# A 64-wide recurrence on TensorE: block-diagonal operands of two heads against 64x64 quarters

## The chip, the core and the metric

The kernel runs on one core of one Trainium2 chip. The metric is the device time in microseconds of one execution. Engines are called TensorE (PE in the profile, its weight loads PEld), VectorE (DVE), ScalarE (ACT), GpSimd (POOL) and SyncE (SP). L229 is line 229 of the kernel before.

## What is computed

One decoder layer over 512 tokens of width 1024: an input projection, two groups of heads side by side (eight RWKV-7 heads of width 64 and eight block-sparse attention heads), an output projection, a layer norm, 32 routed experts and a second norm. The change concerns the RWKV-7 heads, whose reference is a scan over tokens:

```python
def step(S, inp):
    rt, wt, kt, vt, at, bt = inp
    sa = jnp.einsum('bhij,bhj->bhi', S, at)
    S = S * wt[:, :, None, :] + sa[..., None] * bt[:, :, None, :] + vt[..., None] * kt[:, :, None, :]
    yt = jnp.einsum('bhij,bhj->bhi', S, rt)
    return S, yt
```

with `at = -kk`, `bt = kk * a`, and S a 64x64 state per head. All is computed in fp32; the large projections split each operand into two parts.

## The kernel before

The tokens are cut into 8 chunks of 64. Within a chunk the recurrence becomes dense algebra: masked products of the chunk's vectors, the inverse of a unit triangular 64x64 matrix, and products with that inverse; the state then goes from chunk to chunk. Two heads make a pair (`hp`, four of them) and lie on partitions 0 to 63 and 64 to 127.

For each pair there are four stages. `feat` (L399) projects keys, receptances and values (three projections of 24 products with 512 moving columns, L356) and makes the operands AR and BK, held in one of two slots, so that the next pair's may be made while the last is in use. `pre` (L543) works on all 8 chunks: it copies BK into block-diagonal operands (L550 to L554), so that one 128x128 product serves both heads; multiplies (L569, L571) and masks (L572 to L580); inverts the diagonal 16-blocks by substitution, 15 rounds of a shuffle, a product and a sum on VectorE (L583 to L587); transposes the operands on TensorE and copies them out in 64-row pieces, on VectorE and ScalarE (L592 to L605); and doubles the inverse from 16 to 32 and to 64, in two groups of 4 chunks (L616 to L653). L655 to L664 make what the state of each chunk needs. `chain` (L669) runs over the chunks: a transpose of the state, a scaled copy on ScalarE (L683), one product, and additions on VectorE (L688, L689). `gnorm` (L692) normalizes.

All products go through the helper at L229, transposes through L232, whose records carry no other line; which stage one belongs to is seen from its neighbours and its tiles. The program is written stage by stage, and a scheduler lays each engine's instructions in an order by priority. `early` (L725) gives `feat` of the next pair a priority 200 instructions ahead of its place and `pre` one of 100 ahead, so on TensorE the projections of the next pair lie between the products of this one. Each engine then runs its list strictly in order. The work buffers of `pre` are freed at its end and reused by the next pair's. The projections of the attention (L476) and the attention itself (L505) come after; they fill TensorE from about 250 us on. The experts follow from about 500 us.

Of the kernel before, what the change touches and what calls it, by code (L numbers as in the profile page):

```python
# [12 lines left out]
AF = mybir.ActivationFunctionType  # L13
OP = mybir.AluOpType
# [10 lines left out]
    ("tri", 130), ("bdone", 128), ("i64", 64), ("m16d", 64), ("minc", 64),  # L25
    ("mstr", 128), ("m16", 128), ("m32", 128), ("d16", 16), ("bm16", 8), ("hsel", 4),
# [5 lines left out]
def const_array(which):  # L32
# [14 lines left out]
    c["m16d"] = (s[:, None] // 16 == t[None, :] // 16) & (s[:, None] < t[None, :])  # L47
    c["minc"] = s[:, None] <= t[None, :]
    c["mstr"] = same * (s[:, None] < s[None, :])
    c["m16"] = same * ((s[:, None] // 32 == s[None, :] // 32) & (s[:, None] % 32 < 16) & (s[None, :] % 32 >= 16))  # L50
    c["m32"] = same * ((s[:, None] < 32) & (s[None, :] >= 32))
    c["d16"] = (p[:, None] % 16 == np.arange(16)[None, :])
    c["bm16"] = (p[:, None] // 16 == np.arange(8)[None, :])
# [132 lines left out]
def layer(ctx: ExitStack, tc: tile.TileContext, xT, xt, wb, wad, pc, wla, al, gl, cst, cst2, cst3, abias, wout,  # L186
# [199 lines left out]
    CH = [(T(128), T(128)) for _ in range(2)]  # L386
# [155 lines left out]

    def pre(hp, W, RB):  # L543
        d = st[hp]
        AR, BK = v3(d["AR"].f, 8), v3(d["BK"].f, 8)
        BD = [T(1024, *W) for _ in range(2)]
        bd = [v3(t.f, 8) for t in BD]
        at("pa", hp)
        for w in range(2):
            P.memset(bd[w][0:64, :, 64:128], 0.0)  # L550
            P.memset(bd[w][64:128, :, 0:64], 0.0)
            for h in range(2):
                q = slice(64 * h, 64 * h + 64)
                S.activation(bd[w][q, :, q], BK[q, :, 64 * w:64 * w + 64], AF.Copy)  # L554
        T16, T32, RB_, KB_, VB, RH = (T(1024, *W) for _ in range(6))
        AkT = T(1024, *W)
        t16, t32, arb, ark, vb, rh, akt = (v3(t.f, 8) for t in (T16, T32, RB_, KB_, VB, RH, AkT))
        Tc, z, zt = T(128, *W), T(128, *W), T(128, *W)
        tc3, z3, zt3 = (v3(t.f, 8) for t in (Tc, z, zt))
        pr = T(256, *W)  # L560
        P.memset(vb[0:64, :, 64:128], 0.0)
        P.memset(vb[64:128, :, 0:64], 0.0)
        at("pb", hp)
        for g in range(2):
            cs = slice(4 * g, 4 * g + 4)
            pa, pk = bank(RB), bank(RB)
            pa4, pk4 = v3(pa, 4), v3(pk, 4)
            for c in range(4):
                mm(pa4[:, c, :], bd[0][:, 4 * g + c, :], AR[:, 4 * g + c, 0:128])  # L569
            for c in range(4):  # L570
                mm(pk4[:, c, :], bd[1][:, 4 * g + c, :], AR[:, 4 * g + c, 0:128])  # L571
            V.tensor_tensor(v3(pr.f, 4), pa4[:, :, 64:128], bc(cc("m16d"), 4), op=OP.mult)  # L572
            V.tensor_reduce(tc3[:, cs, :], pr.f.rearrange("p (c q t) -> p c t q", c=4, q=4), axis=AX.X, op=OP.add)
            for dst, src, m in ((t16, pa4, "m16"), (t32, pa4, "m32"), (akt, pk4, "mstr")):
                V.tensor_tensor(dst[:, cs, :].rearrange("p c (h t) -> p c h t", h=2),
                                src[:, :, None, 64:128].to_broadcast([128, 4, 2, 64]),
                                cc(m).rearrange("p (h t) -> p h t", h=2)[:, None].to_broadcast([128, 4, 2, 64]),
                                op=OP.mult)
            V.tensor_tensor(arb[:, cs, 0:64], pa4[:, :, 0:64], bc(cc("minc"), 4), op=OP.mult)
            V.tensor_tensor(ark[:, cs, 0:64], pk4[:, :, 0:64], bc(cc("minc"), 4), op=OP.mult)  # L580

        at("pc", hp)
        V.tensor_copy(z3, bc(cc("d16"), 8))  # L583
        for s in range(15):
            V.stream_shuffle(zt3[:, :, s + 1:], tc3[:, :, s + 1:], [16 * (j // 16) + s for j in range(32)])  # L585
            V.tensor_tensor(zt3[:, :, s + 1:], zt3[:, :, s + 1:], z3[:, :, s:s + 1].to_broadcast([128, 8, 15 - s]), op=OP.mult)  # L586
            V.tensor_tensor(z3[:, :, s + 1:], z3[:, :, s + 1:], zt3[:, :, s + 1:], op=OP.add)  # L587
        at("pd", hp)
        for g in range(2):
            cs = slice(4 * g, 4 * g + 4)  # L590

            for src, o, d0, d1 in ((BK, 0, arb, ark), (AR, 64, rh, vb)):  # L592
                pt = bank(RB)
                pt4 = v3(pt, 4)
                for c in range(4):
                    tp(pt4[:, c, :], src[:, 4 * g + c, o:o + 128])
                for w, dst in enumerate((d0, d1)):
                    q = slice(64 * w, 64 * w + 64)
                    for h, o_ in ((0, 0 if dst is vb else 64), (1, 64)):
                        o_ = 0 if dst is rh else o_  # L600
                        qd = slice(64 * h, 64 * h + 64)
                        if h:
                            V.tensor_copy(dst[qd, cs, o_:o_ + 64], pt4[q, :, 64:128])  # L603
                        else:
                            S.activation(dst[qd, cs, o_:o_ + 64], pt4[q, :, 0:64], AF.Copy)  # L605
            pv = bank(RB)
            for c in range(4):
                mm(v3(pv, 4)[:, c, :], akt[:, 4 * g + c, :], vb[:, 4 * g + c, :])
            S.activation(rh[0:64, cs, 64:128], v3(pv, 4)[0:64, :, 0:64], AF.Copy)
            V.tensor_copy(rh[64:128, cs, 64:128], v3(pv, 4)[64:128, :, 64:128])  # L610
        at("pe", hp)
        for t in (AkT, pr, zt, Tc, *BD):
            t.free()
        qg, oh = AR, BK
        bufs, G = [], []
        for g in range(2):  # L616
            cs = slice(4 * g, 4 * g + 4)
            Z, X, Y, WB = T(512, *W), T(512, *W), T(512, *W), T(1024, *W)
            bufs += [Z, X, Y, WB]
            P.tensor_tensor(Z.f.rearrange("p (c q t) -> p c q t", c=4, q=8),  # L620
                            z3[:, cs, None, :].to_broadcast([128, 4, 8, 16]),
                            cc("bm16")[:, None, :, None].to_broadcast([128, 4, 8, 16]), op=OP.mult)
            wb5 = WB.f.rearrange("p (c w h j) -> p c w h j", c=4, w=2, h=2)
            P.memset(wb5[0:64, :, :, 1, :], 0.0)
            P.memset(wb5[64:128, :, :, 0, :], 0.0)
            G.append((g, cs, Z, X, Y, v3(Z.f, 4), v3(X.f, 4), v3(Y.f, 4), wb5, v4(WB.f, 4, 2)))

        def both(banks, work, evac):
            for g, cs, Z, X, Y, z4, x4, y4, wb5, w4 in G:
                ps = B[RB[banks[g]]]  # L630
                for c in range(4):
                    work(v3(ps, 4)[:, c, :], c, 4 * g + c, z4[:, c, :], x4[:, c, :], y4[:, c, :])
                evac(ps, g, Z, X, Y)

        def copy(g, o, i):
            if g == 0:
                S.activation(o, i, AF.Copy)
            else:
                V.tensor_copy(o, i)

        for g, cs, Z, X, *_ in G:
            V.transpose(X.f, Z.f)
        both((2, 0), lambda o, c, k, z, x, y: mm(o, t16[:, k, :], x), lambda ps, g, Z, X, Y: copy(g, Y.f, ps))
        both((1, 2), lambda o, c, k, z, x, y: mm(o, y, z),
             lambda ps, g, Z, X, Y: V.tensor_tensor(Z.f, ps, Z.f, op=OP.add))  # L645
        both((0, 1), lambda o, c, k, z, x, y: mm(o, z, rh[:, k, :], start=(c == 0), stop=False),
             lambda ps, g, Z, X, Y: copy(g, X.f, ps))
        both((2, 2), lambda o, c, k, z, x, y: mm(o, t32[:, k, :], x), lambda ps, g, Z, X, Y: copy(g, Y.f, ps))
        both((0, 1), lambda o, c, k, z, x, y: mm(o, z, y, start=False), lambda *a: None)
        for g, cs, Z, X, Y, z4, x4, y4, wb5, w4 in G:  # L650
            p14 = B[RB[g]].rearrange("p (c w j) -> p c w j", c=4, w=2)
            S.activation(wb5[0:64, :, :, 0, :], p14[0:64], AF.Copy)
            V.tensor_copy(wb5[64:128, :, :, 1, :], p14[64:128])  # L653
        at("pf", hp)
        for g, cs, Z, X, Y, z4, x4, y4, wb5, w4 in G:  # L655
            pq, po = (B[RB[2]], B[RB[0]]) if g == 0 else (B[RB[1]], B[RB[2]])
            for c in range(4):
                mm(v3(pq, 4)[:, c, :], w4[:, c, 0, :], arb[:, 4 * g + c, :])
            for c in range(4):
                mm(v3(po, 4)[:, c, :], w4[:, c, 1, :], arb[:, 4 * g + c, :], stop=False)  # L660
                mm(v3(po, 4)[:, c, :], vb[:, 4 * g + c, :], ark[:, 4 * g + c, :], start=False)
# [4 lines left out]
        for t in bufs + [z, T16, T32, RB_, KB_, VB, RH]:  # L666
            t.free()
# [959 lines left out]
```

## Time and profile before

| | |
|---|---|
| median of 3 runs | 770.71 us (768.93 to 770.89) |
| the profiled execution | 770.63 us, span 768.9 us |
| TensorE busy in the span | 668.0 us, 87% |
| VectorE busy | 429.8 us, 56% |
| ScalarE busy | 250.1 us, 33% |
| GpSimd busy | 193.6 us, 25% |
| TensorE's granted clock, mean | 0.927 of full speed |
| share of the chain of waits: TensorE, VectorE, DMA | 54%, 24%, 17% |

The profile holds one execution. A record of TensorE lasts from its start until its last result, and the next one starts before that, so busy time is more than the time its work needs; the distance from start to start tells the pace. The chain of waits goes back from the last instruction to what released each one. The granted clock is TensorE's, as a share of 2.4 GHz; its lower level is half of that.

### The profile page before, as it was taken

Reading aid. Unit: us, or ns where it says so; the run is one execution under the profiler, and the core shown is the slowest. Engines: PE = TensorE matmul, PEld = TensorE weight load, DVE = VectorE, ACT = ScalarE, POOL = GpSimd, SP = SyncE. Lnnn points to the kernel's source line nnn. Section 1 sums busy time; section 2 is a strip of 40 time slices with the busy share of each in tenths; the row PEclk is TensorE's granted clock in tenths of the full one; section 3 lists DMA queues with packets and bytes.
Section 4 is the critical chain, followed back from the end, with each engine's and each line's share of the span. In section 5 each row is a group of like instructions: output and inputs, shape, how many; then the busy total and the mean of one; then the engine's idle time right before and its main releaser. Section 6 shows DMA issues by size and latency. Waiting matters only on the chain.

```text
span 768.9 us, 9702 instructions
## 1 busy us (share of the span) xinstructions
PE 668.0 (87%) x3420; PEld 421.4 (55%) x3420; DVE 429.8 (56%) x1243; ACT 250.1 (33%) x525; POOL 193.6 (25%) x198
## 2 busy tenths in 40 slices
PE   8988978879889899899999997499999897879870
PEld 2766866677778577667767676333333232223340
DVE  4488588868777985572444498821221121202975
ACT  4333324233333345461453343121322121201330
POOL 3133341353253220310211052611121110101432
PEclk9989999989898999999999997599999998977995
DMA  8611000000100113340637446489999999999603
GB/s 321 256 55 55 29 29 27 29 28 28 28 29 14 56 40 99 93 163 1 246 110 261 181 160 262 160 311 421 427 420 425 425 422 423 423 422 406 258 3 113
DMA packets 28484, 147.18 MB, mean 191 GB/s; under 512 B 5113, under 2 KB 5625, under 8 KB 20492
## 3 DMA queue, kind: packets, MB, share of 16 engines
q1 hardware_dynamic: 23676, 134.61, 45.0%
q0 software_dynamic: 4608, 11.62, 3.9%
q8 instruction: 29, 0.48, 0.3%
q14 instruction: 27, 0.22, 0.1%
q10 hardware_dynamic: 144, 0.26, 0.1%
HBM read 138.38 MB, written 15.36 MB: 200 GB/s over the span
## 4 chain that ended last, share of the span: by engine, by line
PE 54%; DVE 24%; DMA 17%; issue 2%; ACT 1%; POOL 1%; SPq 0%; DVEq 0%; ACTq 0%; POOLq 0%
PE bank L229 49%; DMA b<-in_wex 13%; PE bank L232 4%; DMA a<-in_wex 4%; DVE base L586 2%; DVE base L587 2%; DVE a L147 1%; DVE base L1392 1%; DVE b L603 1%; DVE base L585 1%; DVE a L460 1%; DMA a<-in_xT 1%; DVE base L1214 1%; DVE base L242 1%; DVE base L688 1%
## 5 line engine op out<-in xcount | busy, mean ns | idle before, releaser
L229 PE MATMUL bank<-a,b 128*128 128x512 f32 (+2 forms) x1112 | 286.5, 455 | 12.8 <-DMA a<-in_wex 12.0
L229 PEld LDWEIGHTS bank<-a,b 128*128 128x128 f32 (+1 forms) x1112 | 158.1, 175 | 95.4 <-issue 50.3
L229 PE MATMUL bank<-b,base 128*64 128x512 f32 (+1 forms) x412 | 92.7, 497 | 8.7 <-DMA b<-in_wex 5.1
L337 POOL TENSOR_TENSOR b<-b,b 128x1024 fp32r<-128x1024 f32 x22 | 52.4, 2382 | 131.5 <-ACT b L336 131.2
L1226 DVE SCALAR_TENSOR_TENSOR base<-bank,base 128x256 f32<-128x256 f32 x16 | 7.7, 483 | 126.2 <-ACT base L1225 126.2
L229 PE MATMUL bank<-a,base 128*64 128x512 f32 (+3 forms) x308 | 75.7, 570 | 3.0 <-DMA a<-in_wex 1.9
L229 PEld LDWEIGHTS bank<-b,base 128*64 128x64 f32 (+1 forms) x412 | 41.7, 163 | 47.8 <-issue 34.1
L229 PE MATMUL bank<-a 128*128 128x128 f32 (+4 forms) x248 | 55.6, 333 | 5.5 <-DVE base L243 2.5
L229 PEld LDWEIGHTS bank<-a,base 128*64 128x64 f32 (+2 forms) x308 | 24.3, 143 | 46.8 <-issue 37.3
L1225 ACT ACTIVATE base<-bank 128x256 f32<-128x256 f32 x16 | 6.1, 384 | 132.3 <-PE bank L229 132.3
L229 PEld LDWEIGHTS bank<-a 128*128 128x128 f32 (+1 forms) x248 | 36.0, 190 | 18.3 <-issue 5.3
L229 PE MATMUL bank<-a,a 128*128 128x128 f32 (+2 forms) x200 | 42.6, 346 | 1.4 <-DVE base L243 1.1
L232 PE MATMUL bank<-base 128*128 128x128 f32 x156 | 30.1, 293 | 10.7 <-DVE base L689 5.7
L232 PEld LDWEIGHTS bank<-base 128*128 128x128 f32 x156 | 18.1, 143 | 38.3 <-issue 16.2
L229 PEld LDWEIGHTS bank<-a,a 128*128 128x128 f32 x200 | 32.2, 213 | 8.7 <-issue 5.1
L229 PE MATMUL bank<-base 128*128 128x36 f32 (+4 forms) x136 | 28.3, 344 | 8.4 <-DVE base L1062 3.2
L232 PE MATMUL bank<-base,a 128*128 128x128 f32 x168 | 31.7, 289 | 0.0
L229 PE MATMUL bank<-b,a 128*128 128x128 f32 x192 | 29.9, 298 | 1.7 <-DVE a L645 0.9
L336 ACT ACTIVATE b<-b 128x1024 fp32r<-128x1024 f32 x25 | 26.3, 1055 | 13.5 <-PE bank L229 6.7
L1316 POOL DMA_INDIRECT ydram<-x,base x13 | 13.1, 1011 | 67.1 <-ACT base L1231 56.1
L229 PEld LDWEIGHTS bank<-b,a 128*128 128x128 f32 x192 | 27.0, 211 | 3.9 <-DVE a L645 1.9
L520 DVE CUSTOM_DVE_ANT_0 a<-bank,a 128x512 f32<-128x512 f32 (+3 forms) x32 | 15.6, 488 | 20.9 <-PE bank L232 13.7
(311 smaller groups left out, 1010.5 us busy)
## 6 DMA issues: line engine op xcount, KB each, us to landing
a<-in_wex SPq DMA_DIRECT2D x28, 2048.0 KB, 30.6
b<-in_wex SPq DMA_DIRECT2D x30, 1024.0 KB, 26.5
b<-in_wb SPq DMA_DIRECT2D x25, 512.0 KB, 3.3
a<-in_wex SPq DMA_DIRECT2D x16, 512.0 KB, 15.0
ydram<-base SPq DMA_DIRECT2D x1, 4096.0 KB, 15.2
a<-ydram POOLq DMA_DIRECT2D x4, 1024.0 KB, 14.4
x<-in_wout SPq DMA_DIRECT2D x6, 512.0 KB, 3.8
a<-in_xT SPq DMA_DIRECT2D x8, 256.0 KB, 5.7
```

Source lines behind the costliest of these rows:

```text
L147: ins = f(*args, **kw)
L229: return inorder(PE.matmul(o, l, r, start=start, stop=stop, skip_group_check=True))
L232: return inorder(PE.transpose(o, i, late("ident")))
L242: V.tensor_tensor(t, y, y, op=OP.mult)
L336: S.activation(hi.f, raw.f, AF.Copy)
L337: (V if 0 < k < 4 else P).tensor_tensor(lo.f, raw.f, hi.g, op=OP.subtract)
L460: V.scalar_tensor_tensor(r.f, r.f, pcol(f"rk{hp}"), k2.f, op0=OP.mult, op1=OP.mult)
L520: V.tensor_tensor_reduce(scs[h].f[:, 0:n], ps[:, 0:n], DT.f[:, 512 - n:512], 1.0, -3e38, op0=OP.add, op1=OP.max, accum_out=mx[:, h:h + 1])
L586: V.tensor_tensor(zt3[:, :, s + 1:], zt3[:, :, s + 1:], z3[:, :, s:s + 1].to_broadcast([128, 8, 15 - s]), op=OP.mult)
L587: V.tensor_tensor(z3[:, :, s + 1:], z3[:, :, s + 1:], zt3[:, :, s + 1:], op=OP.add)
L1226: V.scalar_tensor_tensor(hd.f, ph[:, 256:512], GT.f[:, p:p + 1], hd.f, op0=OP.mult, op1=OP.mult)
L1316: P.indirect_dma_start(out=ydram, out_offset=bass.IndirectOffsetOnAxis(ap=IDY.i[:, p:p + 1], axis=0), in_=Y.g, in_offset=None, bounds_chec ...
```

## The change

Products of the recurrence use 64x64 quarters of TensorE, head 0 on rows and columns 0 to 63, head 1 on 64 to 127; `each` issues them in turn. Block-diagonal operands, their copies and memsets are gone. Transposes become products with a 64x64 identity. The diagonal blocks inverted by substitution have 8 rows instead of 16 (7 rounds instead of 15), and one more doubling, from 8 to 16, is added; the doublings run over all 8 chunks at once. ScalarE takes the evictions of the transposes. The states are kept transposed, so that a step of `chain` has no transpose. The masks become `m4` (the 8-blocks and the three doublings), `mk`, `d8` and `bm8`. The core of the diff, with removed lines of `pre` left out, since they stand above:

```diff
+    HS = (slice(0, 64), slice(64, 128))
+
+    def each(work, ks=range(8)):
+        for k in ks:
+            for q in HS:
+                work(k, q)
...
+        at("pb", hp)
         for g in range(2):
...
+            for w, p4 in enumerate((pa4, pk4)):
+                each(lambda c, q: mm(p4[q, c, :], BK[q, 4 * g + c, 64 * w:64 * w + 64], AR[q, 4 * g + c, 0:128]), range(4))
+            V.tensor_tensor(tm[:, cs], pa4[:, :, None, 64:128].to_broadcast([128, 4, 4, 64]),
+                            v3(cc("m4"), 4)[:, None].to_broadcast([128, 4, 4, 64]), op=OP.mult)
+            V.tensor_reduce(tc3[:, cs, :], tm[:, cs, 0, :].rearrange("p c (q t) -> p c t q", q=8), axis=AX.X, op=OP.add)
+            V.tensor_tensor(rb[:, cs], pa4[:, :, 0:64], bc(cc("mk")[:, 0:64], 4), op=OP.mult)
+            V.tensor_tensor(m3[:, cs, 192:320], pk4, bc(cc("mk"), 4), op=OP.mult)
...
+        for s in range(7):
+            V.stream_shuffle(zt3[:, :, s + 1:], tc3[:, :, s + 1:], [8 * (j // 8) + s for j in range(32)])
+            V.tensor_tensor(zt3[:, :, s + 1:], zt3[:, :, s + 1:], z3[:, :, s:s + 1].to_broadcast([128, 8, 7 - s]), op=OP.mult)
             V.tensor_tensor(z3[:, :, s + 1:], z3[:, :, s + 1:], zt3[:, :, s + 1:], op=OP.add)
...
+                pt4 = v4(bank(RB), 4, 2)
+                for w in range(2):
+                    each(lambda c, q: mm(pt4[q, c, w, :], src[q, 4 * g + c, o + 64 * w:o + 64 * w + 64], ident[q, q]), range(4))
+                S.activation(dst, pt4, AF.Copy)
+        pv = v3(bank(RB), 8)
+        each(lambda k, q: mm(pv[q, k, :], ak[q, k, :], vb[q, k, :]))
+        S.activation(rh[:, :, 64:128], pv, AF.Copy)
...
+        P.tensor_tensor(Z.f.rearrange("p (c q t) -> p c q t", c=8, q=8),
+                        z3[:, :, None, :].to_broadcast([128, 8, 8, 8]),
+                        cc("bm8")[:, None, :, None].to_broadcast([128, 8, 8, 8]), op=OP.mult)
+
+        for j in (1, 2):
+            V.transpose(X.f, Z.f)
+            ps = bank(RB)
+            p8 = v3(ps, 8)
+            each(lambda k, q: mm(p8[q, k, :], tm[q, k, j, :], xx[q, k, :]))
+            S.activation(Yt.f, ps, AF.Copy)
+            ps = bank(RB)
+            p8 = v3(ps, 8)
+            each(lambda k, q: mm(p8[q, k, :], yy[q, k, :], zz[q, k, :]))
+            V.tensor_tensor(Z.f, ps, Z.f, op=OP.add)
...
+        for g in range(2):
+            each(lambda c, q: mm(p4[g][q, c, :], zz[q, 4 * g + c, :], rh[q, 4 * g + c, :], start=(c == 0), stop=False), range(4))
+            S.activation(half(X2, g), B[RB[g]], AF.Copy)
+        for g in range(2):
+            ps = B[RB[2]]
+            each(lambda c, q: mm(v3(ps, 4)[q, c, :], tm[q, 4 * g + c, 3, :], x2[q, 4 * g + c, :]), range(4))
+            S.activation(half(Y2, g), ps, AF.Copy)
+        for g in range(2):
+            each(lambda c, q: mm(p4[g][q, c, :], zz[q, 4 * g + c, :], y2[q, 4 * g + c, :], start=False), range(4))
...
+        for k in range(7):
+            each(lambda k, q: mm(ps[q, k, :], bt[q, k, :], w4[q, k, 1, :], start=(k == 0), stop=False), [k])
+            each(lambda k, q: mm(ps[q, k, :], kt[q, k, :], vb[q, k, :], start=False, stop=(k == 6)), [k])
+        V.tensor_tensor(ST[:, 0:7, :], ps[:, 0:7, :], fac.f[:, 8 * hp:8 * hp + 7, None].to_broadcast([128, 7, 64]), op=OP.mult)
         for g in range(2):
...
+            each(lambda c, q: mm(p4[g][q, c, :], w4[q, 4 * g + c, 0, :], m3[q, 4 * g + c, 0:128]), range(4))
...
+        for k in range(8):
+            each(lambda k, q: mm(ps[q, k, :], w4[q, k, 1, :], rb[q, k, :], start=(k == 0), stop=False), [k])
+            each(lambda k, q: mm(ps[q, k, :], vb[q, k, :], rk[q, k, :], start=False, stop=(k == 7)), [k])
+        S.activation(Y, py, AF.Copy)
...
     def chain(hp, cb):
...
+        ps = bank(cb)
         for c in range(1, 8):
-            ps = bank(cb)
-            tp(ps[:, 128:256], SB_.f)
-            S.activation(ST.f, ps[:, 128:256], AF.Copy, scale=fac.f[:, 8 * hp + c - 1:8 * hp + c])
-            mm(ps[:, 0:128], ST.f, qg[:, c, 0:128])
             if c < 7:
-                for h in range(2):
-                    q = slice(64 * h, 64 * h + 64)
-                    V.tensor_tensor(SB_.f[q, q], ps[q, 64:128], oh[q, c, 64:128], op=OP.add)
-            V.tensor_tensor(Y[:, 64 * c:64 * c + 64], ps[:, 0:64], oh[:, c, 0:64], op=OP.add)
+                each(lambda c, q: mm(ps[q, 0:64], qg[q, c, 64:128], ST[q, c - 1, :]), [c])
+            each(lambda c, q: mm(ps[q, 64 * c:64 * c + 64], ST[q, c - 1, :], qg[q, c, 0:64]), [c])
+            if c < 7:
+                V.scalar_tensor_tensor(ST[:, c, :], ps[:, 0:64], fac.f[:, 8 * hp + c:8 * hp + c + 1], ST[:, c, :],
+                                       op0=OP.mult, op1=OP.add)
+        V.tensor_tensor(Y[:, 64:512], ps[:, 64:512], Y[:, 64:512], op=OP.add)
```

## Rows read from the trace of the kernel before

**Rows 1.** Stretches, one per pair: length, engines' busy us, granted clock, DMA share, GB/s.
```profile
44.00:107.00 63.00, 53.94 (x316) 45.62 (x316) 48.48 (x125) 20.58 (x36) 22.80 (x22) 0.93 0.15 51
107.00:170.00 63.00, 52.99 (x325) 42.69 (x324) 51.73 (x152) 21.94 (x43) 23.40 (x26) 0.96 0.08 26
170.00:237.00 67.00, 60.21 (x343) 49.96 (x343) 51.15 (x154) 21.93 (x43) 23.48 (x26) 0.88 0.08 24
237.00:300.00 63.00, 58.10 (x354) 45.58 (x355) 52.29 (x165) 26.25 (x56) 15.65 (x16) 1.00 0.17 55
```

**Rows 2.** The chain of waits, 44 to 315 us, shares by line.
```profile
by line: PE bank L229 47.5%; DVE base L586 6.0%; DVE base L587 4.9%; issue 4.4%; DVE b L603 3.7%; DVE base L585 3.4%; PE bank L232 3.2%; DVE base L688 1.6%; DVE a L460 1.6%; DVE base L242 1.5%; DVE base L243 1.2%; DVE b L610 1.1%; DVE base 
```

**Rows 3.** Groups by line, 107 to 170 us: busy us, mean ns, idle before and its releasers.
```profile
L585 DVE STREAM_SHUFFLE base<-base 128x120 f32<-128x120 f32 (+14 forms) x15 | 3.5, 236 | 0.1
L586 DVE TENSOR_TENSOR base<-base 128x120 f32<-128x120 f32 (+14 forms) x15 | 5.2, 347 | 0.3
L587 DVE TENSOR_TENSOR base<-base 128x120 f32<-128x120 f32 (+14 forms) x15 | 5.5, 368 | 0.3
...
L688 DVE TENSOR_TENSOR base<-bank,a 64x64 f32<-64x64 f32 x12 | 2.6, 221 | 1.1 <-PE bank L229 0.8
...
L683 ACT ACTIVATE base<-bank,base 128x128 f32<-128x128 f32 x7 | 2.5, 363 | 10.2 <-PE bank L232 10.2
...
L645 DVE TENSOR_TENSOR a<-bank,a 128x512 f32<-128x512 f32 x2 | 1.4, 684 | 0.0
...
L664 ACT ACTIVATE a<-bank 128x512 f32<-128x512 f32 x2 | 1.2, 598 | 1.8 <-PE bank L229 1.8
```

**Rows 4.** Line L586, 107 to 170 us: xcount: ns min/median/max, first and last start.
```profile
L586 DVE TENSOR_TENSOR base<-base x15: 174/226/2059, 114.8 to 139.4; 128x120 f32<-128x120 f32 x1, 128x112 f32<-128x112 f32 x1, 128x104 f32<-128x104 f32 x1, 128x96 f32<-128x96 f32 x1
```

**Rows 5.** TensorE's timeline in the doubling of the first pair: start, us, what.
```profile
82.33 2.16 PE L229 MATMUL bank<-b,a 128*128 128x128 f32 x16
84.33 1.06 PE L229 MATMUL bank<-a 128*128 128x128 f32 x8
85.14 1.18 PE L229 MATMUL bank<-a,b 128*128 128x512 f32 x4
86.16 1.07 PE L229 MATMUL bank<-base,a 128*128 128x128 f32 x8
```

**Rows 6.** TensorE's costliest group, 44 to 300 us: busy us, mean ns, idle before.
```profile
L229 PE MATMUL bank<-a,b 128*128 128x512 f32 (+1 forms) x336 | 102.8, 429 | 0.8 <-DVE b L337 0.8
```

**Rows 7.** Waits from 44 to 300 us: in total, times, longest.
```profile
PE bank L229 <- DVE a L460: 10.0, 3, 3.9
```

**Rows 8.** Groups by line and shape on VectorE, 107 to 170 us.
```profile
L585 DVE STREAM_SHUFFLE base<-base 128x56 f32<-128x56 f32 x1 | 0.2, 224 | 0.0
...
L586 DVE TENSOR_TENSOR base<-base 128x8 f32<-128x8 f32 x1 | 0.2, 174 | 0.0
```

**Rows 9.** TensorE's timeline in the attention.
```profile
392.05 0.66 PE L232 MATMUL bank<-base,a 128*128 128x128 f32 x4
392.64 0.86 PE L229 MATMUL bank<-a,b 128*64 128x128 f32 x3
...
393.87 1.09 PE L229 MATMUL bank<-a,b 128*64 128x128 f32 x14
394.88 0.55 PE L232 MATMUL bank<-base,a 128*128 128x128 f32 x3
```

**Rows 10.** TensorE's timeline, 64-column loads with one moving column.
```profile
737.83 0.40 PE L229 MATMUL bank<-a,base 128*64 128x1 f32 x8
```

**Rows 11.** TensorE's timeline, 170 to 237 us: projections and transposes of the third pair.
```profile
176.32 1.26 PE L229 MATMUL bank<-a,b 128*128 128x512 f32 x3
...
180.16 0.27 PE L232 MATMUL bank<-base,a 128*128 128x128 f32 x1
180.19 0.48 PE L229 MATMUL bank<-a,b 128*128 128x512 f32 x1
...
222.30 0.95 PE L229 MATMUL bank<-a,b 128*128 128x512 f32 x3
```

More of the change, by code (lines that the diff above doesn't have):

```diff
@@ L24 @@
 EARLY = [
-    ("tri", 130), ("bdone", 128), ("i64", 64), ("m16d", 64), ("minc", 64),
-    ("mstr", 128), ("m16", 128), ("m32", 128), ("d16", 16), ("bm16", 8), ("hsel", 4),
+    ("tri", 130), ("bdone", 128), ("i64", 64), ("m4", 256), ("mk", 128), ("d8", 8), ("bm8", 8), ("hsel", 4),
 ]
@@ L46, in const_array @@
     c["i64"] = (s[:, None] == t[None, :])
[L47 to L53, printed above, removed]
+    sc, tr = s[:, None], t[None, :]
+    within = lambda n: (sc // (2 * n) == tr // (2 * n)) & (sc % (2 * n) < n) & (tr % (2 * n) >= n)
+    c["m4"] = np.concatenate([(sc // 8 == tr // 8) & (sc < tr), within(8), within(16), within(32)], 1)
+    c["mk"] = np.concatenate([sc <= tr, sc < tr], 1)
+    c["d8"] = (p[:, None] % 8 == np.arange(8)[None, :])
+    c["bm8"] = (s[:, None] // 8 == np.arange(8)[None, :])
     hs = (h[:, None] == np.arange(2)[None, :]).astype(np.float32)
@@ L385, in layer @@
     smls = [T(8), T(8)]
-    CH = [(T(128), T(128)) for _ in range(2)]
     vt = T(2048, BB[6])
@@ L567, in pre @@
             pa4, pk4 = v3(pa, 4), v3(pk, 4)
[L568 to L578, printed above, removed]
@@ L587, in pre @@
+        for s in range(7):
+            V.stream_shuffle(zt3[:, :, s + 1:], tc3[:, :, s + 1:], [8 * (j // 8) + s for j in range(32)])
+            V.tensor_tensor(zt3[:, :, s + 1:], zt3[:, :, s + 1:], z3[:, :, s:s + 1].to_broadcast([128, 8, 7 - s]), op=OP.mult)
             V.tensor_tensor(z3[:, :, s + 1:], z3[:, :, s + 1:], zt3[:, :, s + 1:], op=OP.add)
         at("pd", hp)
+        ident = late("ident")
         for g in range(2):
             cs = slice(4 * g, 4 * g + 4)
[L592 to L610, printed above, removed]
+            for src, o, dst in ((BK, 0, m3[:, cs, 0:256].rearrange("p c (w x) -> p c w x", w=2)[:, :, :, 0:64]),
+                                (AR, 64, rv[:, cs, :].rearrange("p c (w x) -> p c w x", w=3)[:, :, 0:3:2, :])):
+                pt4 = v4(bank(RB), 4, 2)
+                for w in range(2):
+                    each(lambda c, q: mm(pt4[q, c, w, :], src[q, 4 * g + c, o + 64 * w:o + 64 * w + 64], ident[q, q]), range(4))
+                S.activation(dst, pt4, AF.Copy)
@@ L611, in pre @@
+        pv = v3(bank(RB), 8)
+        each(lambda k, q: mm(pv[q, k, :], ak[q, k, :], vb[q, k, :]))
+        S.activation(rh[:, :, 64:128], pv, AF.Copy)
         at("pe", hp)
-        for t in (AkT, pr, zt, Tc, *BD):
+        for t in (zt, Tc):
             t.free()
-        qg, oh = AR, BK
-        bufs, G = [], []
+        Z, X, Yt = (T(512, *W) for _ in range(3))
+        X2, Y2, WB = (T(1024, *W) for _ in range(3))
+        zz, xx, yy = (v3(t.f, 8) for t in (Z, X, Yt))
+        x2, y2, w4 = v3(X2.f, 8), v3(Y2.f, 8), v4(WB.f, 8, 2)
@@ new lines, in pre @@
+        half = lambda t, g: t.f[:, 512 * g:512 * g + 512]
+        p4 = [v3(B[RB[g]], 4) for g in range(2)]
+        for g in range(2):
[5 more added lines that the diff above has]
+            S.activation(half(Y2, g), ps, AF.Copy)
@@ L623, in pre @@
[L623 to L661, printed above, removed]
-            V.tensor_tensor(qg[:, cs, 0:64], v3(pq, 4)[:, :, 0:64], AR[:, cs, 0:64], op=OP.add)
-            V.tensor_tensor(qg[:, cs, 64:128], v3(pq, 4)[:, :, 64:128], bc(cc("i64"), 4), op=OP.add)
-            S.activation(oh[:, cs, :], v3(po, 4), AF.Copy)
@@ L665, in pre @@
+        S.activation(Y, py, AF.Copy)
         at()
-        for t in bufs + [z, T16, T32, RB_, KB_, VB, RH]:
+        for t in (M, TM, RV, z, Z, X, Yt, X2, Y2, WB):
             t.free()
@@ L739, in layer @@
     gnorm(3, GB)
-    for t in (Ce, Gl, SG, fac, *CH[0], *CH[1], *slots[0], *slots[1]):
+    for t in (Ce, Gl, SG, fac, *slots[0], *slots[1]):
         t.free()
```

53 lines of the change are left out of this document (18 added, 35 removed).

## The prediction

> **What bounds it now.** I read the stretches first, then the chain of waits, then the groups of one stretch, then TensorE's own order. The four head pairs follow each other at nearly the same distance, 63, 63, 67 and 63 us [rows 1]. In them TensorE counts as busy 225 of 256 us and VectorE 204, ScalarE only 91; so two engines are nearly full and a third is free. The chain of waits of this part says which of the two ends last [rows 2]: half of it is TensorE (47.5% and 3.2%), but the three lines of the substitution (L585 to L587) hold 14.3% of 271 us, 39 us, the copies of the transposed operands (L603, L610) 4.8%, 13 us, and L688 of the chunk chain 1.6%. The instructions of one pair's 15 rounds sum to 14.2 us [rows 3], but they run from 114.8 to 139.4, 25 us [rows 4]: what lies between is VectorE's other work, the copies L603 and the chunk chain of the pair before among it.
>
> TensorE's busy time is not all multiplication. An fp32 multiplication leaves two records, a transpose one. Sixteen records of 128x128 follow in 2.00 us and the next eight in 0.81 [rows 5], 0.10 to 0.125 each; I take 0.111 us, 0.223 per multiplication. The 336 records of 512 columns in the four stretches [rows 6] take at most 0.25 each (four in 1.02 us [rows 5]), 82 us, the 1002 others of [rows 1] about 0.109 in the mean, 109 us: TensorE has some 190 us of work in the 256. The other 66 are short waits, waits of some us (one kind in [rows 7]) and halved clock, since the granted clock is 0.88 to 1.00 by stretch [rows 1]. So there is room, but TensorE is the next engine in line.
>
> **The change, part by part.** Four head pairs; the sum is made against the profiled execution, 770.6 us (span 768.9), which is the median of the runs to 0.1 us.
>
> (a) Substitution. 15 rounds of three instructions become 7, of widths 56 to 8 columns. Those 21 exist already as the last rounds of the old loop: 0.224 down to 0.174 us each [rows 8], so about 4.1 us in place of 14.2. Of the 39 us on the chain 71% go: -27 us.
>
> (b) Transposes. L603 and L610 (13 us on the chain) leave VectorE; in their place ScalarE does four evictions of 512 columns per pair and one for the product that needs V, 0.60 us each by L664 [rows 3], 3 us per pair. ScalarE is busy 22 us of 63 [rows 1], and the products that need these operands come after the substitution, which hides them. Without that cover they cost up to 12 us. Behind them on ScalarE's queue wait the weight splits L336. Between -13 and -1 I take -8, nearer to the gain, since the old transposes already lie between projections [rows 11], beside the substitution.
>
> (c) Chunk chain. A step was transpose, ScalarE 0.36, product, two additions of 0.22 [rows 3]; it becomes one round on TensorE and one VectorE instruction, and the next step waits for that alone. The four chains also run beside the next pair's substitution, so only what stands on the chain counts: -5, between 0 and -8.
>
> (d) Smaller work. The four ScalarE copies of L554 and ten memsets on POOL go, and the masks of a group lose 512 columns and three instructions, about 1 us by L645 (0.68 for 512 [rows 3]), 2 us per pair. That work starts a pair, once the features are done: -4, between 0 and -10.
>
> (e) TensorE's own time. Before: 88 multiplications and 16 transposes per pair outside the chunk chain, 88 x 0.223 + 16 x 0.109 = 21.4 us. After: 300 multiplications, 96 with 128 moving columns and 204 with 64, alternating between the two diagonal quarters. No row shows a quarter. The nearest are attention's 64-column halves: 14 records start within 0.82 us (393.87 + 1.09 - 0.27 for the last one) [rows 9], two for each 0.109 us plus a lone one at either end; so halves run at once. For 64 moving columns two rows bound a pair: half of 0.109, and the eight 64-column loads with one moving column, 0.2 us between the first start and the last for four pairs, or 0.06 to 0.07 a pair [rows 10]; I take 0.057 us. That makes 48 x 2 x 0.109 + 102 x 2 x 0.057 = 22.1 us, and 16 batches with a lone record at an end add 1.3: 23.4. Plus 2 us per pair, +8. If quarters don't overlap it is 44 us: the upper bound, taken up below.
>
> (f) One more doubling. The blocks of 8 need two doublings where 16 needed one, and the two chunk groups no longer overlap in them. A doubling is transpose about 0.7, product 1.2 with its latency, eviction 0.60, product 1.2, addition 0.68 [rows 3, 5]: 4.4 us, against about 4 us that the second group hid before in part. I take 3.7 us per pair, 15 in all, but projections fill TensorE meanwhile: +8, between 0 and +15.
>
> (g) Changes of form. Projections use the whole array, and the scheduler lays them between the recurrent products: in the third stretch they come in 26 separate runs, of which the first and the last stand in [rows 11], and the other stretches look alike. Today both are 128x128 and nothing is lost. Where the form changes the trace shows a price: from four transposes to 64-column halves 0.20 us from start to start (392.05 + 0.66 - 0.27 to 392.64), and back 0.20 (394.69 to 394.88), where 0.109 is the pace of equal forms; and the four transposes behind such a change last 0.66 where 3 x 0.109 + 0.27 would be 0.60 [rows 9]. A round trip is thus 0.09 + 0.05 + 0.09 + 0.06 = 0.29 us. 26 a pair make 30 us; where TensorE would wait anyway this is free. I take half, +15, between 0 and +40.
>
> DMA is 8 to 17% in these stretches [rows 1], and no load is moved; the constants shrink. The expert part after 500 us begins earlier by whatever is gained, as its loads wait for buffers that the attention frees; I move it as a block.
>
> Sum: -27 - 8 - 5 - 4 = -44; + 8 + 8 + 15 = +31; together -13, so 757.5 us. As a check, that takes 13 of the 31 us that [rows 1] leave TensorE not busy; it can't go much beyond them.
>
> **Rivals.** First, TensorE fills up: the changes of form are all on the path and more numerous. For it: a free VectorE makes recurrent products ready while projections are too, and the old order already lays single records between single projections [rows 11]; each then also loses its partner. Against it: most of the old runs are several records long. At 26 round trips all exposed, the sum is 30 - 15 = 15 worse, +2; from there on it is slower. At 40 a pair, 47 us in (g), +19: 790 us.
>
> Second, quarters don't overlap. For it: no row shows two products on different rows of the array at once; attention's halves share all 128. Then (e) is 96 x 0.218 + 204 x 0.112 = 44 us a pair, 22 more than before, so TensorE would need some 280 us in 256: -44 + 90 + 8 + 15 = +69, 840 us; where idle time takes a third of the 69, 817. Against it: the halves write two halves of one bank at once already [rows 9], and the diagonal quarters share neither rows nor columns. The Trainium skill, TensorEngine Tiling (Gotcha 1: PSUM Pressure), speaks for this rival: different row tiles can't access the same PSUM bank at the same time, and the change writes both quarters into one bank; no run here shows whether that holds for quarters in different columns.
>
> Third, VectorE was holding up more than its own share. With some 15 us per pair gone from it by (a) to (d), the features of the next pair end earlier, the waits of TensorE for L460 (10 us [rows 7]) and the like go with them, and the changes of form fall into waits: -44 + 8 + 8 - 16 = -44, about 727 us. Against it: TensorE's 190 us of work, 198 by (e), have to fit into 212 then, 93% of the time.
>
> Fourth, gains and costs cancel, 768 to 773.
>
> **How the numbers follow.** The forecast with its own bounds (735 to 767) has 0.5. The third rival has 0.16. The fourth has 0.06. The first has 0.20 and the second 0.08, as the pairs of halves speak against it. A measurement of this kernel tells 0.3%, 2.3 us, from no change: faster 0.66, same 0.06, slower 0.28. For 8 of 10 the range goes from 724 to 790: 0.10 lies above, the second rival and a little of the first, and some 0.06 below.
>
> **What would show it.** Right: 21 records of the substitution in place of 45, about 4 us of VectorE per pair and under 12 us from first to last; TensorE records with 64 rows and 64 columns whose starts lie 5 to 10 ns apart in twos; gaps of 0.2 us where they meet 512-column projections; pairs about 60 us apart or less, with TensorE's lines over 60% of the chain. Wrong: quarter records that follow each other singly at 0.056 or 0.11 us (second rival); more than 40 runs of projections per pair with gaps at each (first); pairs 50 us apart (third). The sum fails if the doublings on ScalarE and VectorE, not TensorE, turn out to be what a pair waits for, or if the granted clock of the stretches falls below 0.88, since I assumed that quarter products hold it as full ones do.

## The result: slower, 4.2%

| | before | after |
|---|---|---|
| median of four runs of each | 770.35 us | 799.92 us (799.52 to 810.8) |
| profiled execution, span | 770.63, 768.9 us | 799.52, 797.6 us |
| TensorE busy | 668.0 us, 87% | 715.7 us, 90% |
| VectorE busy | 429.8 us, 56% | 349.8 us, 44% |
| granted clock, mean | 0.927 | 0.947 |

The ratio is 1.0421, interval 1.0332 to 1.051. The forecast was 757.5 us, with a range of 724 to 790: wrong in sign, and above the range. One run below, the slowest of e2's four, fell in a slower state of the chip and is left out of its median and its ratio. Lines of the kernel after differ from those of before: the helper of all products is L227, transposes L230, the substitution L574 to L576, the first masks L565.

The stretches of [rows 1] for the kernel after:

```profile
44.00:107.00 63.00, 59.98 (x593) 41.66 (x593) 22.59 (x61) 13.14 (x21) 9.81 (x6) 0.97 0.14 43
107.00:170.00 63.00, 61.11 (x721) 43.23 (x719) 29.80 (x89) 15.46 (x26) 12.78 (x10) 0.97 0.07 18
170.00:237.00 67.00, 65.11 (x755) 45.49 (x755) 31.18 (x91) 17.10 (x28) 15.14 (x11) 1.00 0.09 25
237.00:300.00 63.00, 59.84 (x639) 39.83 (x641) 28.09 (x77) 12.82 (x20) 14.42 (x9) 1.00 0.11 31
```

VectorE (the third busy time of a row) went from 204 us of these 256 to 112, TensorE (the first) from 225 to 246, at a clock no lower than before. The pairs no longer end where these stretches do: the first masks of a pair stand at 46.5, 131.8, 203 and 274 us, so a pair lasts 71 us and more where it lasted some 64. The chain of waits, 44 to 330 us, answers to [rows 2]:

```profile
by line: PE bank L227 70.1%; issue 15.6%; POOL b L335 3.3%; ACT b L334 1.9%; DVE base L449 1.1%; DVE b L443 1.1%; DVE a L447 1.0%; DVE b L576 0.9%; DVE a L434 0.8%; POOL a L445 0.7%; PE bank L230 0.6%; DVE a L443 0.5%; POOL a L687 0.4%; DVE
```

Of the substitution's three lines one is left in this row, with 0.9%; the copies of transposed operands are gone. In their place stand TensorE, from 50.7% to 70.7%, and "issue", from 4.4% to 15.6%: time in which an engine waits for nothing that the profile shows. The waits of TensorE and of its weight loads, 44 to 320 us, say whose. First the kernel before (the highest four of the twelve rows of PE, together 30.1 us, 28.6 of them for VectorE, and then a row of PEld):

```profile
PE bank L229 <- DVE a L460: 10.0, 3, 3.9
PE bank L232 <- DVE base L689: 5.7, 7, 2.5
PE bank L229 <- DVE base L243: 3.6, 2, 2.5
PE bank L229 <- DVE b L603: 3.5, 2, 2.5
...
PEld bank L229 <- issue: 12.9, 42, 1.3
```

and the kernel after (the highest three of seven rows, together 10.8 us):

```profile
PE bank L227 <- DVE base L449: 3.8, 3, 1.3
PE bank L227 <- DVE a L464: 2.5, 1, 2.5
PE bank L227 <- DVE a L434: 1.4, 3, 0.5
...
PEld bank L227 <- issue: 51.6, 206, 1.5
```

So the relief of VectorE did reach TensorE: its waits fell by 19 us. But its weight loads now stop 206 times while they wait for nothing that the profile shows, 0.25 us each, 51.6 us in place of 12.9. Nearly all of these stops (203 of the 206, counted in the trace) stand where a quarter product meets a product over the whole array. Those 39 us less the 19, with the 8 us that the prediction gave for the quarters' own work, are 28; measured were 29.6. That the two meet so well is partly chance: the stretch holds a little less of the program after than before, the partners lost in the timeline below (7 us) are left out, and so is the clock. The granted clock from 44 to 300 us was 0.94 before and 0.99 after. Eight records of 128 columns last 1.06 us in [rows 5]; at the lower level of the clock, in the kernel before, they last 1.91:

```profile
168.03 1.91 PE L229 MATMUL bank<-a,a 128*128 128x128 f32 x8
```

By the clock of [rows 1] and of the rows above, TensorE spent some 30 us at the lower level before and 8 after, so up to 11 us came back there (an estimate). The kernel after is slower in spite of its clock. Where the stops stand is seen in the timeline of TensorE and its weight loads:

```profile
88.14 0.43 PE L227 MATMUL bank<-base,b 64*64 64x128 f32 x2
88.49 0.19 PEld L227 LDWEIGHTS bank<-a,b 128*128 128x128 f32 x1 [0.17 <-issue]
88.49 0.49 PE L227 MATMUL bank<-a,b 128*128 128x512 f32 x1
...
88.92 0.19 PEld L227 LDWEIGHTS bank<-a,a 64*64 64x64 f32 x2 [0.24 <-issue]
88.92 0.33 PE L227 MATMUL bank<-a,a 64*64 64x64 f32 x2
89.17 0.19 PEld L227 LDWEIGHTS bank<-a,b 128*128 128x128 f32 x1
89.17 0.50 PE L227 MATMUL bank<-a,b 128*128 128x512 f32 x1
89.60 0.19 PEld L227 LDWEIGHTS bank<-a,a 64*64 64x64 f32 x2 [0.25 <-issue]
```

One projection product of the next pair, one quarter product (two records, as fp32 needs), one projection product: 0.68 us from the first to the next (88.49 to 89.17). In a run a 512-column record takes 0.23 (e5's run of 24, below), and a quarter product that has its partner beside it half of 0.116, so 0.40 us are lost in each round, 0.06 of them the lost partner's and 0.34 the change's. The scheduler has laid 177 runs of quarter products into the recurrent part (counted in the compiled order; in the trace 116 of them hold a single product), 44 a pair, most likely because the two sides now become ready together. In the kernel before both sides have the same form.

### The profile page after: what moved, and what is told of

Read it like the earlier page. It is cut to its first block, busy times and chain, and to the rows that moved or that the text cites. A ratio compares the mean times of both kernels' runs of the same rounds, so it can differ in the third digit from the quotient of the medians.

```text
span 797.6 us, 12803 instructions
## 1 busy us (share of the span) xinstructions
PE 715.7 (90%) x5176; PEld 426.1 (53%) x5176; DVE 349.8 (44%) x991; ACT 230.4 (29%) x465; POOL 163.0 (20%) x138
## 4 chain that ended last, share of the span: by engine, by line
PE 62%; DMA 16%; DVE 12%; issue 6%; POOL 2%; ACT 1%; DVEq 0%; ACTq 0%; SPq 0%; POOLq 0%
PE bank L227 58%; DMA b<-in_wex 12%; DMA a<-in_wex 4%; PE bank L230 3%; DVE a L145 1%; DVE base L1366 1%; POOL b L335 1%; ACT b L334 1%; DVE base L1188 1%; DVE base L449 1%; DVE base L145 1%; DVE base L759 0%; DVE b L443 0%; DVE a L447 0%; DVE b L576 0%
## 5 line engine op out<-in xcount | busy, mean ns | idle before, releaser
L227 PE MATMUL bank<-a,b 128*128 128x512 f32 (+4 forms) x1288 | 304.7, 419 | 5.5 <-DMA a<-in_wex 5.5
L227 PEld LDWEIGHTS bank<-a,b 128*128 128x128 f32 (+2 forms) x1288 | 163.6, 164 | 96.0 <-issue 54.6
L227 PE MATMUL bank<-a 64*64 64x64 f32 (+5 forms) x720 | 81.5, 269 | 5.4 <-POOL a L448 1.5
L227 PE MATMUL bank<-a,base 128*64 128x512 f32 (+2 forms) x280 | 75.8, 644 | 7.7 <-DMA a<-in_wex 7.6
L227 PE MATMUL bank<-b,base 128*64 128x512 f32 x256 | 64.6, 624 | 9.0 <-DMA b<-in_wex 9.0
L227 PEld LDWEIGHTS bank<-a 64*64 64x64 f32 (+2 forms) x720 | 53.8, 148 | 31.8 <-issue 17.7
L227 PE MATMUL bank<-a,a 64*64 64x64 f32 (+3 forms) x440 | 65.8, 275 | 0.2 <-ACT a L626 0.2
L227 PEld LDWEIGHTS bank<-a,a 64*64 64x64 f32 (+1 forms) x440 | 38.9, 144 | 23.4 <-issue 20.7
L227 PEld LDWEIGHTS bank<-a,base 128*64 128x64 f32 (+1 forms) x280 | 21.4, 148 | 54.3 <-issue 41.0
L227 PEld LDWEIGHTS bank<-b,base 128*64 128x64 f32 x256 | 17.9, 141 | 42.3 <-issue 36.6
L227 PE MATMUL bank<-base 128*128 128x36 f32 (+4 forms) x136 | 28.0, 342 | 6.6 <-DVE base L1036 3.3
L230 PEld LDWEIGHTS bank<-base 128*128 128x128 f32 x128 | 14.1, 144 | 28.1 <-issue 16.2
L227 PE MATMUL bank<-x 128*128 128x512 f32 (+4 forms) x96 | 18.6, 306 | 10.2 <-POOL x L1080 8.0
L230 PE MATMUL bank<-base 128*128 128x128 f32 x128 | 21.8, 291 | 5.1 <-DVE base L1200 3.9
L517 DVE CUSTOM_DVE_ANT_0 a<-bank,a 128x512 f32<-128x512 f32 (+3 forms) x32 | 15.6, 489 | 23.3 <-PE bank L230 12.8
L347 DVE SCALAR_TENSOR_TENSOR a<-bank,base,a 128x511 f32<-128x511 f32 x10 | 7.5, 749 | 40.6 <-ACT a L346 40.6
L227 PE MATMUL bank<-base,b 64*64 64x128 f32 (+1 forms) x384 | 22.6, 256 | 0.0
```

Of the source, the lines that this page charges most:

```text
L227: return inorder(PE.matmul(o, l, r, start=start, stop=stop, skip_group_check=True))
L230: return inorder(PE.transpose(o, i, late("ident")))
L347: V.scalar_tensor_tensor(o[:, 1:], ps[:, 0:511], pcol(col), o[:, 1:], op0=OP.mult, op1=OP.add)
L517: V.tensor_tensor_reduce(scs[h].f[:, 0:n], ps[:, 0:n], DT.f[:, 512 - n:512], 1.0, -3e38, op0=OP.add, op1=OP.max, accum_out=mx[:, h:h + 1])
```

## Experiments

Theory A: a change of form, from the whole array to quarters and back, costs a third of a microsecond, all of it on the path, and the order by the scheduler makes 177 of them; the rest of the change does what it says. The rivals B are named in each. All times are medians, all ratios against runs of the kernel before on the same chip, three rounds each. Where two changed kernels are compared they may have run on different chips; the medians of the kernel before on these chips lie between 770.35 and 772.14 us.

**e1: projections later.** In the changed kernel:

```diff
-    FO, GO, PO, CO = 200, 0, 100, 0
+    FO, GO, PO, CO = 0, 0, 100, 0
```

> The changed kernel, with the features of the next pair no longer placed 200 instructions ahead (one number). TensorE's list then has 88 runs of quarter products in the recurrent part, where the changed kernel has 177. Theory A (changes between full-array and quarter products fill TensorE, 0.34 us a round trip as the changed kernel's trace shows): 89 x 0.34 = 30 us less, about 770 us. Rival B (the serial steps of a pair set the time and the changes of form lie in waits): the features come later, the next pair starts later, 805 to 830 us.

Measured 775.09 us, 1.005 [1.0022, 1.0077] of before: 25 us less than after. The stops of weight loads, 44 to 320 us, fell by 125, to

```profile
PEld bank L227 <- issue: 28.0, 81, 1.5
```

that is by 23.6 us, close to the gain. The two need not meet: of the 116 lone products 17 are left (counted in the trace), while the granted clock from 44 to 300 us is lower, 0.94 against 0.99. A is borne out, 5 us above its number.

**e8: the same edit in the kernel before,** as a control.

> Control for e1: the kernel before with the same change of the scheduler's priorities (projections of the next pair at their own place, 0 in place of 200 ahead). Its products all use the whole array but for the attention's, so no changes of form are saved. Theory A (e1 won by fewer changes of form): 766 to 776, no gain. Rival (the later place of the projections is better in itself): 745 to 755, the 25 us of e1.

Measured 771.55 us, 1.0022 [0.9994, 1.005]: no gain. What e1 won is not a better place of the projections in itself.

**e2: TensorE's order by hand.** `feat`, `pre`, `chain` and `gnorm` of the changed kernel become generators that hand over at each `yield`; a driver calls them in turn, and TensorE keeps that order. The first projections of the attention move up into the last pair. Its core:

```diff
-        early(FO, feat, j)
-        early(GO, gnorm, j - 1, GB)
-        early(PO, pre, j, W, RB)
-        early(CO, chain, j, CB_)
...
+        for _ in range(7):
+            step(P_)
+            step(C)
+        drain(C)
+        step(F)
+        step(N)
+        step(J, 12)
+        step(P_)
...
```

> The changed kernel's arithmetic with TensorE's order of the recurrent part written out: the products of a batch stay together, projections come in blocks of 4 to 24 records where a batch waits; 26 runs of quarter products in place of 177. Theory A: 151 x 0.34 = 51 us less than the changed kernel, 749 us, faster than the kernel before. Rival B: no fewer waits, and a fixed order adds some, 800 us or more.

Measured 756.69 us (756.51 to 762.0), 0.9849 [0.9785, 0.9912]: A, though 8 us above its number. The products are those of the changed kernel, one for one. TensorE now waits in four places of a pair; of the second pair, 118 to 177 us:

```profile
PE bank L227 <- ACT a L439: 1.8, 1, 1.8
PE bank L227 <- DVE a L707: 1.4, 1, 1.4
PE bank L227 <- DVE a L609: 1.1, 1, 1.1
PE bank L227 <- ACT base L666: 0.7, 1, 0.7
```

**e5: those waits filled.** The driver of e2, with projections put into three of them:

```diff
-        for _ in range(7):
+        step(P_)
+        step(C)
+        if C:
+            step(J, 2)
+        step(P_)
+        step(C)
+        step(P_)
+        if C:
+            step(J, 3)
+        step(C)
+        for _ in range(4):
             step(P_)
             step(C)
...
+        step(F)
         step(P_)
         step(N)
+        step(J, 4)
         step(F)
```

> The order by hand of e2, with projections moved into three waits that TensorE still had in each pair: 1.8 us before the 2-column products of the key norms, 1.05 us before the second half of the first products, 1.44 us before the third step of the chunk chain. 32 runs of quarter products in the recurrent part in place of 26. Theory A (TensorE's list is the bound, and its waits and changes of form add up): 3 x 1.8 us and 3 x 2.5 us less, 6 x 0.34 us more, so 748 us, between 745 and 752. Rival (a pair is held by its chain through VectorE and ScalarE, and the waits only move): 757 to 762.

Measured 746.32 us (745.51 to 747.77), 0.9703 [0.9662, 0.9743]: A. Three of the four rows are gone, and only the fourth is left of them in a pair. This version is faster than both kernels: 24 us below the one before, 54 below the one after. Its pairs are 53 us apart (first masks at 108.7, 161.9 and 215.0 us).

**e9: changes of form put back, nothing else.** In e5 twelve pairs of projection products follow the last quarter products of a head pair in one run. Here they are laid between those quarter products:

```diff
+            yield "s"
...
+            yield "y"
...
-        drain(P_)
+        while step(P_):
+            if more:
+                step(J, 1)
```

> e5 with the last twelve pairs of projection products of a head pair, which stood in one run behind its last quarter products, laid one pair at a time between those quarter products (four or so calls each). Work, operands and every other place in the order stay; TensorE changes form 36 times more there and back in the recurrent part (68 runs of quarters in place of 32). Theory A (0.34 us for each there and back, as read off the changed kernel's trace): 746 + 12 = 758, between 754 and 761. Rival (the changed kernel is slow through waits that the scheduler's order makes, and a change of form costs next to nothing by itself): 745 to 749.

Measured 755.91 us, 0.9807 [0.9751, 0.9863]: 9.6 us more than e5 for 36 more trips, 0.27 us each. Part of e9's timeline:

```profile
151.59 0.73 PE L227 MATMUL bank<-a,b 128*128 128x512 f32 x2
152.25 0.33 PE L227 MATMUL bank<-a,a 64*64 64x64 f32 x4
152.41 0.28 PE L227 MATMUL bank<-a 64*64 64x64 f32 x4
152.63 0.73 PE L227 MATMUL bank<-a,b 128*128 128x512 f32 x2
```

The same work in e5, quarters and then projections in a run:

```profile
149.75 0.28 PE L227 MATMUL bank<-a,a 64*64 64x64 f32 x4
149.86 0.28 PE L227 MATMUL bank<-a 64*64 64x64 f32 x4
149.98 0.28 PE L227 MATMUL bank<-a,a 64*64 64x64 f32 x4
...
155.30 5.76 PE L227 MATMUL bank<-a,b 128*128 128x512 f32 x24
```

A round of e9 is 1.04 us (151.59 to 152.63). In e5 the two quarter products of each row of four records take 0.116 us, so the four of a round 0.23, and two projection products at most 0.48 (24 in 5.76): at least 0.33 us lost in the timeline, of which 0.27 reach the end. Against the kernel before, each on its own chip, the two differ by 0.0104 or 8.0 us, which is 0.22 for a trip, and their intervals do not meet; the price is thus some 0.22 to 0.27. This is the cleanest evidence: no product was added, no partner lost, and the granted clock (0.99) is the same from 44 to 300 us, in e5 and then in e9:

```profile
44.00:300.00 256.00, 241.18 (x3219) 193.42 (x3220) 143.48 (x399) 87.42 (x155) 66.05 (x44) 0.99 0.18 57
```

```profile
44.00:300.00 256.00, 242.35 (x3171) 186.06 (x3172) 139.06 (x391) 79.72 (x142) 60.79 (x41) 0.99 0.16 49
```

**e3 and e4: dummies in the kernel before.** 64 products ahead of the transposes of L596, on one quarter in e3, on the whole array in e4:

```diff
+                    mm(pt4[0:64, c, 0:64], src[0:64, 4 * g + c, o:o + 64], late("ident")[0:64, 0:64])
...
+                    mm(pt4[:, c, 0:64], src[:, 4 * g + c, o:o + 128], late("ident")[:, 0:64])
```

> The kernel before, with one useless 64x64 product put ahead of each of the 64 transposes of the recurrent operands (it is overwritten by the transpose). Theory A: 64 round trips at 0.34 and 0.06 of work, 26 us, the most of it on the path: 785 to 796, and at least 8 us more than the next run. Rival B: 4 us of work beside the substitution, 770 to 775, no slower than the next run.

> The same 64 useless products over all 128 rows and columns of the array (two records of 0.111 us each, 14 us in all, no change of form). Theory A: 772 to 783, below the run with quarters. Rival B: as slow as the run with quarters or slower.

Measured 791.34 us for e3, 1.0262 [1.0222, 1.0302], and 786.07 for e4, 1.0184 [1.0139, 1.0229]. The quarters cost more, by 5.3 us where at least 8 were expected, and e4 misses its number. Its 64 products cost 14.2 us against their control, 0.22 each, a whole multiplication as in [rows 5]: nothing of it was hidden. So the difference of the two says of the price of a change only that it is above zero. e3 alone says a little more: its 64 products cost 19.5 us, 0.30 each; if a lone quarter's 0.116 lay on the path as fully as e4's products did, 0.19 are left for there and back, less than in e9. In e3 most trips (51 of the 64, counted in the trace) start behind a product or transpose of 128 columns, not of 512. What the pair does show is that in the kernel before, too, TensorE's additional work lay on the path in full.

**e7: 16-blocks again, in the changed kernel.** 15 rounds of substitution, one doubling less:

```diff
-        for s in range(7):
+        for s in range(15):
...
-        for j in (1, 2):
+        for j in (2,):
```

> The changed kernel as it stands (scheduler's order), with 16-blocks again: 15 rounds, one doubling less. VectorE gets 10 us more per pair. The compiled order has 120 runs of quarter products in the recurrent part in place of 177. Theory A (each run costs 0.3 us, VectorE is off the path): 57 x 0.3 = 17 us and 8 us of TensorE's work less than 800, so 775, between 768 and 783. Rival (substitution on the path): 800 to 825.

Measured 785.54 us, 1.0188 [1.0137, 1.0238]: 14 us less than after, 3 above A's range. Fewer products and stops (166 in place of 206) gain more than VectorE's additional rounds cost. What those rounds cost is not separated: the granted clock from 44 to 300 us is lower too, 0.95 against 0.99.

**e6: 16-blocks again, in e5.** The same edit, the other places of TensorE's order kept.

> e5 with the substitution of before: 16-blocks, 15 rounds, one doubling in place of two; the order of the rest is kept. VectorE gets some 10 us more per pair, TensorE 64 quarter records less per pair (1.9 us) and 8 runs of quarters less in all (2.7 us). Theory A (TensorE is the bound, what VectorE was relieved of is off the path): 735 to 748, not slower than e5. Rival (the shorter substitution is what the pair waits for): 10 to 25 us slower than e5, 758 to 775.

Measured 761.6 us, 0.9893 [0.9863, 0.9923]: 15.3 us more than e5, and here the rival is right. The waits of TensorE in e6, 44 to 300 us, the highest:

```profile
PE bank L227 <- ACT a L439: 12.3, 3, 4.3
PE bank L227 <- DVE b L335: 6.4, 1, 6.4
```

The first row is new, 12.3 us. The granted clock from 44 to 300 us fell as well, from 0.99 in e5 to 0.93, while fewer products and runs gave time back; so the 12.3 us are not simply a share of the 15.3, and what the clock's fall cost is not separated. In e6's timelines of VectorE and of TensorE the last sum of the substitution comes first, then the shifted sum of the keys (L347), which the keys' square (L439) on ScalarE and the 2-column products of their norms wait for:

```profile
132.78 0.17 DVE L620 TENSOR_TENSOR b<-b 128x8 f32<-128x8 f32 x1
...
137.12 0.74 DVE L347 SCALAR_TENSOR_TENSOR a<-bank,base,a 128x511 f32<-128x511 f32 x1
```

```profile
132.58 2.11 PE L227 MATMUL bank<-a,b 128*128 128x512 f32 x8
138.73 1.12 PE L227 MATMUL bank<-x,a 128*128 128x2 f32 x8 [4.04 <-ACT a L439]
```

The eight rounds more stand ahead of L347 in VectorE's list. So the shorter substitution with its additional doubling gains 15 us in e5's order, which e6 keeps, and loses 14 where TensorE's list is full of changes of form (e7).

**e10 and e11: the order by hand in the kernel before.** Is e5's gain the order's alone? `pre` and `chain` of before cut in the same places, the driver that of e5 with projections in twos between the first products and the steps of the chain; in e11 the chain's scaled copy and additions go ahead on the lists of ScalarE and VectorE:

```diff
+            tc.cur_priority -= 400
             if c < 7:
                 for h in range(2):
                     q = slice(64 * h, 64 * h + 64)
                     V.tensor_tensor(SB_.f[q, q], ps[q, 64:128], oh[q, c, 64:128], op=OP.add)
```

> Control for e2 and e5: the kernel before, block-diagonal operands and 16-blocks as they are, with TensorE's order written out by hand in the same places as in e5 (the chunk chain beside the first products, projections in twos between them, the rest as there). Theory A (e5 is fast because the change itself pays once its changes of form are few; the scheduler's order was no burden to the kernel before): 755 to 780. Rival (e5's gain is the order's, and the kernel before would have it too): 740 to 750, as e5.

> e10 with the additions and the scaled copy of the chunk chain ahead of the substitution on VectorE's and ScalarE's lists (a priority 400 earlier); e10 lost 40 us of TensorE to waits for the chain's additions. Theory A (the change itself pays, not the order alone): those 40 us go and little else, 775 to 790, above e5 by 30 or more. Rival (an order by hand gives the kernel before what it gave the changed one): under 755.

Measured 823.09 us, 1.0676 [1.0645, 1.0708], and 821.87, 1.0643 [1.0596, 1.0691]: outside A's numbers, and the rival falls. In e10 TensorE waited 40 us for the chain's additions (L744). In e11 that fell to 14.8 and VectorE's other work took its place, 44 to 340 us:

```profile
PE bank L229 <- DVE a L691: 16.9, 4, 5.5
PE bank L229 <- DVE b L649: 15.9, 4, 5.4
PE bank L232 <- DVE base L747: 14.8, 24, 0.9
PE bank L229 <- DVE base L706: 8.1, 3, 2.8
```

L691 transposes the blocks that the substitution has just inverted, L649 copies transposed operands, L706 copies out the solved blocks. VectorE of before cannot follow this order; that of the change can. It is one order, though, made for the other kernel: whether another would make the kernel before faster than the scheduler's stays open.

## Why the prediction was wrong

**(g), the changes of form, is the step that failed,** in its count and in its share, not in its kind. The price of 0.29 us a trip, read off the attention's halves [rows 9], is near: e9 gives 0.22 to 0.27. The count of 26 was that of the runs of projections in the old order [rows 11], the order of a kernel whose recurrent products waited for VectorE; in the new order both sides alternate, and there are 44 a pair. "Half of them hidden" failed too: the time went with the count all the way, 32 runs in 746 us, 68 in 756, 88 in 775, 177 in 800 (e5, e9, e1, after; between e9 and e1 the order differs in more than this, and e2's 26 runs took 757 us with the waits that e5 fills). 177 x 0.27 are 48 us in place of 15, 33 of the 42 us between the forecast and the result; at 0.22 they are 39, and 24 of the 42. The 116 lone products add half of 0.116 each, 7 us. The first rival had the mechanism, the place, the lost partners and, at 40 trips, 790 us, and its sign, more than 40 runs a pair with gaps at them, is what the trace shows. I gave it 0.20, on the ground that most old runs were several records long (59 of 102 in the four stretches, but 10 of 29 in the first, counted in the trace); that is the very thing which the change undid.

**(a) to (d), VectorE's relief, are right in size on the engine; as terms of the sum they were not measured one by one.** The substitution takes 4.1 us, as forecast, and 137.0 to 141.9 us for its first and last shuffle where 25 us lay. Groups by line, one pair, answering to [rows 3], with the evictions of (b) below:

```profile
L574 DVE STREAM_SHUFFLE b<-b 128x56 f32<-128x56 f32 (+6 forms) x7 | 1.4, 200 | 0.0
...
L576 DVE TENSOR_TENSOR b<-b 128x56 f32<-128x56 f32 (+6 forms) x7 | 1.4, 193 | 0.2
L575 DVE TENSOR_TENSOR b<-b 128x56 f32<-128x56 f32 (+6 forms) x7 | 1.3, 187 | 0.1
```

```profile
L587 ACT ACTIVATE a<-bank 128x512 f32<-128x512 f32 x4 | 2.4, 597 | 8.4 <-PE bank L227 8.4
```

Most of the 44 us came from shares of the chain. In the kernel after, only 19 us of TensorE's waits went. The waits that the view lists are not the whole relief, though, if (e) and (f) hold: with (g) at 48 us and 7 for the lost partners the prediction's own sum is -44 + 8 + 8 + 48 + 7 = +27, 798 us (789 at 0.22 a trip), where 800 were measured; with 19 in place of 44 it would be 823 (814). What else came back, the clock's share among it, no run separates. The check against the 31 us that [rows 1] leave TensorE idle was made with the net of the sum, -13, and so could not warn: e4's cost on TensorE's list came in full in spite of that idle time.

**(e), the quarters' own work, holds in its pace.** A batch of 16 products of 64 columns in the kernel after:

```profile
66.51 1.15 PE L227 MATMUL bank<-b 64*64 64x64 f32 x32
```

32 records start within 0.88 us (1.15 less 0.27 for the last one), some 0.057 for a pair of records, the value taken between [rows 9] and [rows 10]. The second rival falls: one after the other they would take twice that. Both quarters write one bank here. The Trainium skill, TensorEngine Tiling (Array Packing) (Gotcha 1: PSUM Pressure), would have row tiles keep to banks of their own; for diagonal quarters this trace doesn't agree.

**(f), the additional doubling,** was not measured alone; e7 undid it together with the substitution, and e6 shows that the exchange of the two pays 15 us net in e5's order. **The third rival** needed TensorE at 93%; it is at 96% in [rows 1]'s stretches, and spends it on changes. Its 727 us were not reached by e5 either, where 73 stops remain (21.9 us, against 51.6 after):

```profile
PEld bank L227 <- issue: 21.9, 73, 0.8
```

With e5's 32 trips at 0.27, 9 us, the prediction's own sum would have been -44 + 8 + 8 + 9 = -19, 752 us; e5 took 746. The terms fit the change, then, and not the order in which it ran.

## What to carry to other kernels

Where a change gives part of TensorE's products another form than their neighbours', count the places at which the new order lets both meet, not those of the old one, and price each there and back at what a row of a change between the same neighbours shows. Relief of a second engine reaches the time only through the first one's list: here 19 us of listed waits went, and 39 us of stops came. If an order by priority alternates two forms, write the order out, or move one side's priority: here that turned 4.2% slower into 3.0% faster.

## What the runs showed that was not expected

A change of form appears as a stop of the weight load: 0.24 and 0.25 us of "issue" ahead of a quarter's load that follows a 512-column product (88.92 and 89.60 us above), and 0.17 on the way back (88.49). Between equal forms the next load runs beside the product: in e5 above 24 projection products follow within 5.76 us, 0.24 each at most. The Trainium skill, TensorEngine Tiling (Array Packing) (Key Properties), states that a switch of tiling mode drains TensorE; the trace agrees: the load at 88.92 starts 0.43 us behind the product of 88.49, and the price of both ways, 0.22 to 0.27 us, is e9's.

A quarter product alone takes as long as those of both heads together: behind a change of form two records last 0.33 us in the kernel after (88.92) and four last 0.33 in e9 (152.25). A quarter product without its partner throws half away.
